# Weighting expert rows on ScalarE and adding them to the residual by accumulating DMAs, in place of two loads and VectorE additions

## Chip, cores and metric

The kernel runs on one core of a Trainium2 chip. The metric is the device time of one execution in microseconds (us). The time before is 1383.6 us, the median of three runs.

## What is computed

The reference is a two-layer decoder trunk for 256 tokens of width 1024, all in float32: a pooling mixer and a dense SwiGLU, then a gated DeltaNet and a mixture of experts, each added to a residual, and a last RMSNorm. The change touches the mixture of experts alone:

```
logits = t @ router_w + router_b                 # 256 tokens, 8 experts
top_vals, top_idx = top_k(logits, 2);  top_w = softmax(top_vals)
gates = sum(one_hot(top_idx) * top_w)            # (256, 8), two weights a row
for e in range(8):
    y = (silu(t @ w_gate[e]) * (t @ w_up[e])) @ w_down[e]     # inner width 3584
    out = out + gates[:, e:e+1] * y
h = h + out
```

## The kernel before

A float32 product is made of three passes of the faster fp32r format: each 128x1024 half of a weight tile is split into a rounded part `whi` (a cast on ScalarE) and a remainder `wlo` (a subtraction on VectorE, in `split`), and TensorE multiplies hi by hi, hi by lo and lo by hi. The pools of `whi` and `wlo` hold four halves each. Weight tiles of 1 MB come in through SyncE's queue into a ring of 16 raw tiles (six named `raw`, nine `raw_s`, one `raw_t`).

The experts are sorted by how many tokens chose them. When the counts allow it (`fit`, a branch at run time), the first four experts are computed on 128 gathered tokens each and the last four on 64 each (`FEW, SLIM = 4, 64`). An expert has seven chunks of 512 hidden columns. A chunk is a list of jobs, one for each weight half: eight for gate and up (`gate_up`), and four for down (`down`) that are run one chunk later, behind the gate and up jobs of the next chunk. Where an expert is 64 wide, hi and lo of the hidden rows lie side by side in one stationary tile, so a down job is four matmuls whose two halves land in rows 0 to 63 and 64 to 127 of PSUM bank `y0` or `y1`, and the two must be added.

`run` goes through the jobs in a loop: it first emits the split of job i + 3, then the matmuls of job i, then whatever was hung on job i with `after`. The class `Lane` keeps every engine's instructions in the order in which the program emits them (DMAs started from queues other than SyncE's are left out of that). So the copy that `put` makes of a finished expert stands in ScalarE's queue between two weight casts, and its addition stands in VectorE's queue between two subtractions:

```
ahead(i + 3)                   # cast on ScalarE, subtraction on VectorE
jobs[i][2](parts_.pop(i))      # matmuls
for f in post.pop(i, ()):      # put, where, fetch, gain, ...
    f()
```

`where(e)` finds out, by two small matmuls, in which row of a store in DRAM (`kept_rows`) each of the expert's rows belongs: a token's first choice in rows 1 to 256, its second choice in rows 257 to 512, empty rows beyond. `put(e, q)` runs for q = 0 behind the last down job of experts 0 to 6 and for q = 1 at the same job or two jobs later. It copies half q of the expert's output from PSUM to an SBUF tile `rows`; a 64-wide expert's second part is then added by VectorE. After q = 1 GpSimd scatters the tile to the store by an indirect DMA. In expert 7, behind chunks 3 and 4, `fetch(k)` loads the stored first and second choices through SyncE's queue into a raw tile, and `gain(k, tt)` adds them to the residual `h`, multiplied by the tokens' weights `w1` and `w2`, one VectorE instruction for each half of the tokens. Expert 7 itself is added to `h` by `scatter` at the end. `weights` makes the weights `w1`, `w2` and `gate` early in expert 0, one job ahead of the first `where`.

Of the kernel before, what the change touches and what calls it, by code (L numbers as in the profile page):

```python
# [9 lines left out]
F32 = mybir.dt.float32  # L10
F32R = mybir.dt.float32r
I32 = mybir.dt.int32
AF = mybir.ActivationFunctionType
ALU = mybir.AluOpType
# [3 lines left out]
P = 128  # L18
D = 1024
T = 256  # L20
# [194 lines left out]
def trunk(ctx: ExitStack, tc, x, gcol, win, prm, bc, cst, eye, pre, moe, out):  # L215
    nc = tc.nc
    held = {"on": False}
    pe, act, dve, pool, sp = [Lane(tc, e, held) for e in (nc.tensor, nc.scalar, nc.vector, nc.gpsimd, nc.sync)]
# [11 lines left out]
    kept_rows = store.tile([2 * T + 1 + P, D], F32, name="rows")  # L230

    h = cp.tile([P, 2, D], F32, name="h")
# [10 lines left out]
    HQ = [slice(0, 512), slice(512, 1024)]  # L243
# [32 lines left out]
    mhalf = cp.tile([P, 16], F32, name="mhalf")  # L276
# [11 lines left out]
    def raw_tile(dtype=F32):  # L288
        return wp.tile([P, UNIT], dtype, name="raw", bufs=RAWS["r"])
# [16 lines left out]
    def unit(src, i, dma=1, lo_engs=(None, None)):  # L306
        raw = load(src, i, dma)
        return [half(raw, s, lo_engs[s]) for s in range(2)]
# [263 lines left out]
    with esf:  # L572
# [30 lines left out]
        for j in range(1, 10):  # L603
            pg, pu_ = [(second, second_up)[k] if j == 1 else unit(pre, U_FFN + 3 * j + k) for k in range(2)]
# [6 lines left out]
        pg, pu_ = [unit(pre, U_FFN + 30 + k) for k in range(2)]  # L611
# [44 lines left out]
    kept = {}  # L656
# [579 lines left out]
    state, sel, xg, yps, cols = {}, {}, {}, {}, {}  # L1236

    def ms_bank(shape):
        return mps.tile(shape, F32, name="ms", bufs=2)

    def gu_bank(shape=(P, 512)):
        return mps.tile(list(shape), F32, name="gu", bufs=4)
# [4 lines left out]
    def half_mm(o, x_, s, hf, part, at, n, qs=(0, 1)):  # L1247

        (xh_, xl_), (hi, lo) = x_[hf], part
        for q in qs:  # L1250
            k, a = (at % 2) * 2 + q, slice(q * 512, q * 512 + 512)
            mm3(o, xh_[:, k, s], xl_[:, k, s], hi[:, a], lo[:, a], at == q == 0, at == n - 1 and q == 1)

    def sm(name, n=8):
        return mp.tile([P, 2, n], F32, name=name)
# [7 lines left out]
    m1, m2, ed, den, w1, w2 = [six[:, i] for i in range(6)]  # L1263
    lg, o1, o2, l2, gate, g2, rf = [sm(n_) for n_ in ("lg", "o1", "o2", "l2", "gate", "g2", "rf")]
# [112 lines left out]
    def width(e):  # L1377
        return state["width"].get(e, P)
# [37 lines left out]
    def where(e):  # L1416

        n = width(e)
        pw = ms_bank([P, 8])[:n]
        for tt in range(2):  # L1420
            pe.matmul(pw, state["Sp", e][:, tt, cols[e]], tid[:, tt, :], start=tt == 0, stop=tt == 1)
        spare = econ[:n, 6:7]
        dve.scalar_tensor_tensor(spare, pw[:, e:e + 1], 0.0, econ[:n, 3:4], op0=ALU.is_equal, op1=ALU.mult)
        dve.tensor_tensor(slot[:n, e:e + 1], spare, pw[:, e:e + 1], op=ALU.add)

    def put(e, q):
        if q == 0:
            state["put"] = state["rows"].tile([P, D], F32, name="rows", bufs=2)
        n, r, y = width(e), state["put"], yps[e][q]
        if n == P:  # L1430
            act.copy(r[:, HQ[q]], y)
        else:
            act.copy(r[:n, HQ[q]], y[n:2 * n])
            dve.tensor_add(r[:n, HQ[q]], r[:n, HQ[q]], y[:n])
        if q == 1:
            pool.indirect_dma_start(kept_rows, bass.IndirectOffsetOnAxis(ap=slot[:n, e:e + 1], axis=0), r[:n], None)

    def fetch(k):
        r = raw_tile().rearrange("p (t n) -> p t n", t=2)
        sp.dma_start(r, kept_rows[1 + k * T:1 + (k + 1) * T, :].rearrange("(t p) n -> p t n", t=2))  # L1440
        state["kept", k] = r

    def gain(k, tt):
        dve.scalar_tensor_tensor(h[:, tt], state["kept", k][:, tt], (w1, w2)[k][:, tt], h[:, tt], op0=ALU.mult, op1=ALU.add)

    def row_tile(dtype=F32):
        return state["tmp"].tile([P, 512], dtype, name="hm", bufs=2)
# [1 line left out]
    def opened(pg, n=P):  # L1449
        hm = row_tile()  # L1450
        act.activation(hm[:n], pg[:n], AF.Silu)
        return hm
# [83 lines left out]
    def expert_steps(block, few=0):  # L1536

        jobs, post = [], {}

        def after(i, f, *a):  # L1540
            post.setdefault(i, []).append(lambda: f(*a))

        def gate_up(e, c):
            at = len(jobs)
            dense = e == c == block == 0
            for i in range(4 if dense else 0, 8):
                w_, hf, s = i // 4, i // 2 % 2, i % 2

                def mm(part, w_=w_, hf=hf, s=s):
                    if hf == s == 0:  # L1550
                        state[e, w_] = gu_bank()
                    half_mm(state[e, w_][:width(e)], xg[e], cols[e], hf, part, 2 * hf + s, 4)
                jobs.append(((e, c * 4 + max(c - 1, 0) * 2 + 2 * w_ + hf), s, mm))

            def opening_():
                state["sg"] = opened(state[e, 0], width(e))

            def hidden():
                state["hm", e, c] = gated(state.pop("sg"), state[e, 1], width(e))
            if not dense:  # L1560
                after(at + 4, opening_)
            after(len(jobs) - 1, hidden)
            return at

        def down(e, c):
            at = len(jobs)
            base = (c + 2) * 4 + c * 2 if c < NCH - 1 else NCH * 4 + (NCH - 1) * 2
            final = e == NE - 1 and c == NCH - 1
            for fc in range(4):
                def mm(part, fc=fc):  # L1570
                    if c == fc == 0:
                        yps[e] = [mps.tile([P, 512], F32, name=f"y{q}") for q in range(2)]
                    st, sp_ = c == 0 and fc == 0, c == NCH - 1 and fc == 3
                    if final and fc == 3:
                        last_mm(e, c, part)
                    else:
                        down_mm(e, c, fc, part, (0, 1), st, sp_)
                jobs.append(((e, base + fc // 2), fc % 2, mm))
            if c == NCH - 1:
                for q in range(2):  # L1580
                    if not final and not block:
                        after(at + (3, 3 if e == 1 else 5)[q], put, e, q)
                    elif not final:
                        after(at + (3, 5)[q], out_split, e, q)
                        for tt in range(2):
                            after(at + (5, 7)[q], scatter, e, tt, q)
                if final:
                    for q in range(2):
                        for tt in range(2):
                            after(at + 3, scatter, e, tt, q)  # L1590
                    after(at + 3, lambda: close(state["g"]))
            return at

        def turn(e, c):
            state["hid", e, c] = hidden_T(state.pop(("hm", e, c)), (e, c) == (NE - 1, NCH - 1), width(e))

        prev, cut = None, 0
        for e in range(NE):
            for c in range(NCH):
                if (e, c) == (2, 0) and not block:  # L1600
                    after(len(jobs) - 3, turn, *prev)
                    down(*prev)
                    prev, cut = None, len(jobs)
                    for k in range(2):
                        after(cut + 4 + 4 * k, where, 2 + k)
                at = gate_up(e, c)
                if prev is not None:
                    after(at + (3 if c != 1 or e == 0 else TURN), turn, *prev)
                    down(*prev)
                if e % 2 == 1 and c == NCH - 1 and (block or e > 1) and e < NE - 1 - (few and 2):  # L1610
                    es_ = range(e + 1, NE if few and e + 1 == NE - few else e + 3)
                    after(at + 4, choose, es_)
                    for k, kc in zip((6, 7, 8, 9, 9, 10, 11, 11), range(KC)):
                        after(at + k, gather, es_, kc)
                    for k, e_ in enumerate(es_):
                        stays = block or e_ == NE - 1
                        after(at + 13 + 16 * k, back if stays else where, e_)
                if e == NE - 1 and not block and c in (3, 4):
                    after(at + 2, fetch, c - 3)
                    for tt in range(2):  # L1620
                        after(at + 8 + 2 * tt, gain, c - 3, tt)
                prev = e, c
        after(len(jobs) - 3, turn, *prev)
        down(*prev)
        return jobs, post, cut
# [188 lines left out]
```

## Time and profile before

| | |
|---|---|
| median of three runs | 1383.6 us (1383.38 to 1385.76) |
| the profiled execution | 1383.05 us, of which its span is 1381.3 us |
| granted TensorE clock | 0.996 of full speed |
| busy: TensorE / VectorE / ScalarE / GpSimd | 98% / 85% / 71% / 8% of the span |
| weights and the rest read from HBM | 420.11 MB, 309 GB/s over the span |

A matmul of 512 columns shows as 0.39 us long but the next one begins 0.23 us later, since matmuls overlap. An engine's record begins when it has what it waited for, so a late partner shows as a gap ahead of it.

### The profile page before, as it was taken

To read this page: it belongs to the slowest core of one execution; us is meant where nothing else is said; L and a number is where in the kernel's file an instruction comes from. 1 tells how busy PE (TensorE), PEld (TensorE's weight loads), DVE (VectorE), ACT (ScalarE), POOL (GpSimd) and SP (SyncE) were. 2 spreads that over 40 slices of the span, in tenths; PEclk is the share of its full clock that TensorE was granted. 3 is DMA by queue.
4 is the path that set the end of the run, shared out by engine and by line. 5 is a ranking of instruction groups with operands and counts; after the bars stand their busy time and mean duration, and the time that the engine had idled before them with its cause. 6 is when DMAs were issued, how large, how long until landed. Compare 5 with 4: busy or idle time off the path is not lost.

```text
span 1381.3 us, 19930 instructions
## 1 busy us (share of the span) xinstructions
PE 1349.6 (98%) x7149; PEld 1065.4 (77%) x7149; DVE 1171.3 (85%) x1473; ACT 983.0 (71%) x1298; POOL 114.4 (8%) x73
## 2 busy tenths in 40 slices
PE   8999999999998999999899999999999999999996
PEld 8999998989987888888788888876666666666654
DVE  5655556687888899999799999989999999999997
ACT  5544445752475787887688888788888888888875
POOL 0000001122331000000000000000004002201301
PEclk9999999999999999999999999999999999999999
DMA  9355551733319999999799999989999999997593
GB/s 384 153 214 187 195 196 63 292 121 100 116 58 390 395 371 376 379 382 374 304 360 376 374 373 382 376 335 386 404 389 406 421 408 406 413 409 294 230 428 158
DMA packets 60939, 427.51 MB, mean 310 GB/s; under 512 B 6880, under 2 KB 7136, under 8 KB 10400
## 3 DMA queue, kind: packets, MB, share of 16 engines
q1 hardware_dynamic: 59584, 422.75, 77.8%
q0 software_dynamic: 816, 2.88, 0.6%
q8 instruction: 58, 0.95, 0.3%
q10 hardware_dynamic: 432, 0.53, 0.1%
q14 instruction: 49, 0.40, 0.1%
HBM read 420.11 MB, written 6.03 MB: 309 GB/s over the span
## 4 chain that ended last, share of the span: by engine, by line
PE 89%; DVE 6%; issue 2%; ACT 1%; POOL 1%; DMA 0%; SPq 0%; ACTq 0%; POOLq 0%; DVEq 0%
PE gu L203 59%; PE y L203 17%; PE ya L203 9%; DVE wlo L203 4%; PE yq L203 2%; PE tp L203 1%; PE ms L203 1%; ACT whi L203 1%; PE gs L203 1%; DVE raw L203 0%; DVE h L203 0%; DVE rows L203 0%; DMA h<-in_x 0%; DVE hm L203 0%; DVE xl L203 0%
## 5 line engine op out<-in xcount | busy, mean ns | idle before, releaser
L203 DVE TENSOR_TENSOR wlo<-raw,whi 128x1024 fp32r<-128x1024 f32 x345 | 415.0, 1224 | 82.2 <-ACT whi L203 76.6
L203 DVE TENSOR_TENSOR wlo<-raw_s,whi 128x1024 fp32r<-128x1024 f32 x378 | 452.5, 1218 | 33.2 <-ACT whi L203 22.3
L203 ACT CAST whi<-raw_s 128x1024 fp32r<-128x1024 f32 x378 | 392.1, 1053 | 72.5 <-PE gu L203 54.1
L203 ACT CAST whi<-raw 128x1024 fp32r<-128x1024 f32 x346 | 357.9, 1051 | 106.4 <-PE gu L203 73.0
L203 PE MATMUL gu<-whi,xgh 128*128 128x512 f32 (+1 forms) x896 | 356.0, 397 | 3.6 <-DVE tl L203 3.6
L203 PE MATMUL gu<-wlo,xgh 128*128 128x512 f32 (+1 forms) x896 | 352.4, 393 | 3.2 <-DVE wlo L203 3.2
L203 PE MATMUL gu<-whi,xgl 128*128 128x512 f32 (+1 forms) x896 | 351.5, 392 | 0.0
L203 PEld LDWEIGHTS gu<-wlo,xgh 128*128 128x128 f32 (+1 forms) x896 | 144.9, 162 | 69.2 <-DVE wlo L203 15.5
L203 PEld LDWEIGHTS gu<-whi,xgh 128*128 128x128 f32 (+1 forms) x896 | 144.8, 162 | 60.5 <-issue 3.9
L203 PEld LDWEIGHTS gu<-whi,xgl 128*128 128x128 f32 (+1 forms) x896 | 144.8, 162 | 58.0
L203 PE MATMUL y<-wlo,th 128*128 128x512 f32 x328 | 128.9, 393 | 0.5 <-DVE wlo L203 0.3
L203 PE MATMUL y<-whi,th 128*128 128x512 f32 x328 | 128.4, 391 | 0.2 <-ACT th L203 0.2
L203 POOL DMA_INDIRECT rows<-rows,cmi x7 | 57.2, 8165 | 792.4 <-ACT rows L203 499.8
L203 PE MATMUL y<-whi,tl 128*128 128x512 f32 x336 | 113.1, 391 | 0.0
L203 PE MATMUL gu<-xh,wlo 128*128 128x256 f32 x320 | 90.1, 282 | 0.8 <-DVE wlo L203 0.8
L203 PE MATMUL gu<-xh,whi 128*128 128x256 f32 x320 | 90.2, 282 | 0.1
L203 PE MATMUL gu<-xl,whi 128*128 128x256 f32 x320 | 90.1, 281 | 0.0
L203 PEld LDWEIGHTS y<-wlo,th 128*128 128x128 f32 x328 | 61.7, 188 | 16.0 <-DVE wlo L203 3.8
L203 PEld LDWEIGHTS y<-whi,tl 128*128 128x128 f32 x336 | 63.1, 188 | 13.6
L203 PEld LDWEIGHTS y<-whi,th 128*128 128x128 f32 x328 | 61.6, 188 | 13.7 <-ACT th L203 0.6
L203 PEld LDWEIGHTS gu<-xh,wlo 128*128 128x128 f32 x320 | 61.4, 192 | 1.0 <-DVE wlo L203 1.0
L203 PEld LDWEIGHTS gu<-xh,whi 128*128 128x128 f32 x320 | 60.1, 188 | 0.6 <-ACT whi L203 0.3
(390 smaller groups left out, 1740.4 us busy)
## 6 DMA issues: line engine op xcount, KB each, us to landing
raw_s<-in_moe SPq DMA_DIRECT2D x189, 1024.0 KB, 7.1
raw<-in_moe SPq DMA_DIRECT2D x126, 1024.0 KB, 7.1
raw<-in_pre SPq DMA_DIRECT2D x56, 1024.0 KB, 4.9
raw_t<-in_moe SPq DMA_DIRECT2D x20, 1024.0 KB, 7.4
rows<-AB SPq DMA_DIRECT2D x2, 1024.0 KB, 6.5
raw<-rows SPq DMA_DIRECT2D x2, 1024.0 KB, 12.3
gbc<-in_bc SPq DMA_DIRECT2D x3, 512.0 KB, 9.1
h<-in_x SPq DMA_DIRECT2D x2, 512.0 KB, 4.1
```

The lines of the kernel that those rows point to most:

```text
L203: r = f(*a, **k)
```

## The change

Each stored row is multiplied by its weight before it is stored. `where` gets two more small matmuls, which pick the weights of the expert's rows out of `gate` in full float32, and a VectorE copy of them to a column of `mhalf`. `put` applies that column as the scale of ScalarE's activation: a 128-wide expert's copy out of PSUM becomes a scaled copy; for a 64-wide expert the copy and the addition stay and a scaled copy in place follows. `fetch` becomes a DMA of GpSimd's queue that adds 1 MB of the store to `h`, once for each choice, and `gain` is dropped.

```diff
         dve.tensor_tensor(slot[:n, e:e + 1], spare, pw[:, e:e + 1], op=ALU.add)
+        pg = ms_bank([P, 8])[:n]
+        for tt in range(2):
+            pe.matmul(pg, state["Sp", e][:, tt, cols[e]].bitcast(F32), gate[:, tt, :], start=tt == 0, stop=tt == 1)
+        dve.tensor_copy(mhalf[:n, 9 + e:10 + e], pg[:, e:e + 1])
 
     def put(e, q):
         if q == 0:
             state["put"] = state["rows"].tile([P, D], F32, name="rows", bufs=2)
-        n, r, y = width(e), state["put"], yps[e][q]
+        n, r, y = width(e), state["put"][:, HQ[q]], yps[e][q]
+        w = mhalf[:n, 9 + e:10 + e]
         if n == P:
-            act.copy(r[:, HQ[q]], y)
+            act.activation(r, y, AF.Copy, scale=w)
         else:
-            act.copy(r[:n, HQ[q]], y[n:2 * n])
-            dve.tensor_add(r[:n, HQ[q]], r[:n, HQ[q]], y[:n])
+            act.copy(r[:n], y[n:2 * n])
+            dve.tensor_add(r[:n], r[:n], y[:n])
+            act.activation(r[:n], r[:n], AF.Copy, scale=w)
+        r = state["put"]
         if q == 1:
             pool.indirect_dma_start(kept_rows, bass.IndirectOffsetOnAxis(ap=slot[:n, e:e + 1], axis=0), r[:n], None)
 
     def fetch(k):
-        r = raw_tile().rearrange("p (t n) -> p t n", t=2)
-        sp.dma_start(r, kept_rows[1 + k * T:1 + (k + 1) * T, :].rearrange("(t p) n -> p t n", t=2))
-        state["kept", k] = r
-
-    def gain(k, tt):
-        dve.scalar_tensor_tensor(h[:, tt], state["kept", k][:, tt], (w1, w2)[k][:, tt], h[:, tt], op0=ALU.mult, op1=ALU.add)
+        pool.dma_start(h, kept_rows[1 + k * T:1 + (k + 1) * T, :].rearrange("(t p) n -> p t n", t=2), accum_op=ALU.add)
...
                 if e == NE - 1 and not block and c in (3, 4):
                     after(at + 2, fetch, c - 3)
-                    for tt in range(2):
-                        after(at + 8 + 2 * tt, gain, c - 3, tt)
```

## Rows read from the trace of the kernel before

**Rows 1.** The page: busy us, share of the span, instructions of two engines.

```profile
PE 1349.6 (98%) x7149; PEld 1065.4 (77%) x7149; DVE 1171.3 (85%) x1473; ACT 983.0 (71%) x1298; POOL 114.4 (8%) x73
```

**Rows 2.** Windows: us, busy by engine (instructions), clock, DMA share, GB/s.

```profile
1266.40:1281.10 14.70, 14.64 (x65) 8.93 (x64) 14.70 (x17) 13.20 (x17) 8.62 (x1) 1.00 0.13 56
1173.70:1264.90 91.20, 91.20 (x403) 56.51 (x403) 87.91 (x84) 75.44 (x83) 7.70 (x1) 1.00 1.01 408
1297.50:1335.20 37.70, 34.45 (x151) 20.63 (x150) 36.98 (x36) 28.70 (x32) 0.00 (x0) 1.00 1.01 426
```

**Rows 3.** Timeline of TensorE, last down job behind expert 6's rows.

```profile
1280.65 0.39 PE L203 MATMUL y<-whi,th 128*128 128x512 f32 x1
1281.13 0.50 PE L203 MATMUL y<-wlo,th 128*128 128x512 f32 x1
```

**Rows 4.** Total waits of TensorE on VectorE's remainders, from 690 us on.

```profile
PE gu L203 <- DVE wlo L203: 3.2, 4, 1.1
```

**Rows 5.** Groups of VectorE from 450 us on: the additions of `gain`.

```profile
L203 DVE SCALAR_TENSOR_TENSOR h<-raw,six,h 128x1024 f32<-128x1024 f32 x4 | 5.1, 1269 | 0.0
```

**Rows 6.** Timeline of ScalarE where expert 6's rows are copied.

```profile
1266.60 0.58 ACT L203 COPY rows<-y 64x512 f32<-64x512 f32 x1
1267.09 2.00 ACT L203 CAST whi<-raw_s 128x1024 fp32r<-128x1024 f32 x2
1268.98 0.58 ACT L203 COPY rows<-y 64x512 f32<-64x512 f32 x1
1269.46 1.06 ACT L203 CAST whi<-raw_s 128x1024 fp32r<-128x1024 f32 x1
```

**Rows 7.** Timeline of VectorE in the same stretch.

```profile
1267.53 1.21 DVE L203 TENSOR_TENSOR wlo<-raw_s,whi 128x1024 fp32r<-128x1024 f32 x1
1268.67 0.67 DVE L203 TENSOR_TENSOR rows<-rows,y 64x512 f32<-64x512 f32 x1
1269.27 2.34 DVE L203 TENSOR_TENSOR wlo<-raw_s,whi 128x1024 fp32r<-128x1024 f32 x2
1271.54 0.67 DVE L203 TENSOR_TENSOR rows<-rows,y 64x512 f32<-64x512 f32 x1
```

**Rows 8.** Groups of ScalarE, whole span: count, busy us, mean ns, idle before.

```profile
L203 ACT COPY rows<-y 64x512 f32<-64x512 f32 x6 | 3.5, 584 | 0.1
...
L203 ACT ACTIVATE raw<-raw,st 128x512 f32<-128x512 f32 x2 | 1.3, 713 | 0.5 <-POOL st L203 0.5
```

**Rows 9.** Timeline of TensorE at a `where` of a 64-wide expert.

```profile
969.29 0.40 PE L203 MATMUL y<-wlo,th 128*128 128x512 f32 x1
...
969.61 0.47 PE L203 MATMUL y<-whi,th 128*128 128x512 f32 x1
```

**Rows 10.** Timeline of TensorE at `back(7)`: four matmuls in full float32.

```profile
989.53 0.39 PE L203 MATMUL gu<-whi,xgl 128*64 128x512 f32 x1
...
990.43 0.44 PE L203 MATMUL gu<-whi,xgh 128*64 128x512 f32 x1
```

**Rows 11.** Timeline around the first `where`: its matmuls, and `weights` on VectorE.

```profile
461.78 0.39 PE L203 MATMUL ms<-tid,Sp 128*128 128x8 f32 x2 [0.19 <-DVE tid L203]
...
462.02 0.48 PE L203 MATMUL gu<-whi,xgh 128*128 128x512 f32 x1
...
462.52 0.17 DVE L203 TENSOR_TENSOR gate<-gate,g 128x16 f32<-128x16 f32 x1
```

**Rows 12.** Timeline of GpSimd: the scatters of expert 3 and expert 6.

```profile
943.91 1.33 POOL L203 DMA_INDIRECT rows<-rows,cmi  x1 [120.76 <-ACT rows L203]
...
1272.48 17.32 POOL L203 DMA_INDIRECT rows<-rows,cmi  x1 [91.09 <-DVE rows L203]
```

**Rows 13.** Waits of SyncE's queue from 1200 us on: the scatter ahead of `fetch`.

```profile
SPq L203 <- DMA rows<-rows,cmi: 29.7, 1, 29.7
```

**Rows 14.** The page's DMA issues: count, KB each, us to landing.

```profile
raw<-rows SPq DMA_DIRECT2D x2, 1024.0 KB, 12.3
```

**Rows 15.** Timeline of VectorE: expert 7 is added to `h`.

```profile
1370.14 2.07 DVE L203 SCALAR_TENSOR_TENSOR h<-gu,gate,h 128x512 f32<-128x512 f32 x3
```

## The prediction

> **What bounds the kernel now.** I read the page first: TensorE is busy for 98% of the span, VectorE for 85% [rows 1]. That is an average over layers, so I cut the experts into windows. In a 64-wide expert between its seams TensorE has no idle time at all (91.20 of 91.20 us) and VectorE has 3.3 us of 91.2 to spare [rows 2]: TensorE bounds, with VectorE close behind. At the seam to the next expert, where `put` adds its two halves, the order turns: VectorE is busy for 14.70 of 14.70 us [rows 2]. The timeline of TensorE shows what that means: at the last down job of that stretch the second matmul begins 0.48 us after the first, where 0.23 us is usual, because its remainder is only just done [rows 3]. So VectorE's slack at a 64-wide seam is nil, and whatever delays VectorE there delays TensorE by as much. The seams behind experts 4 and 5 show the same sequence as the one behind expert 6; there are three. The third place is the stretch of `gain` in expert 7: 34.45 of 37.70 us of TensorE, so 3.25 us idle, against VectorE at 36.98 us [rows 2]. The list of waits agrees: 3.2 us in four waits on the remainders [rows 4].
>
> **What the removal gives.** The four additions took VectorE 5.1 us [rows 5] and made TensorE wait 3.2 us [rows 4]; the rest was in VectorE's slack. Without them the 3.2 us go: bounds 2.5 us, if a part of the lag comes from elsewhere, and 3.3 us, all the idle time of that window. The two loads gave SyncE's queue a wait of 29.7 us for the scatter [rows 13], with the weight loads behind it. This cost nothing: the DMA share fell to 0.13 [rows 2] while ScalarE's casts went on from the ring. So its removal gives nothing either.
>
> **What the scaled copies cost.** For the four 128-wide experts a copy becomes a scaled copy, once for once, on an engine with slack: nothing; without that cover eight times 713 - 584 ns [rows 8], 1.0 us. For the three 64-wide experts a third instruction stands in ScalarE's queue, and it waits for VectorE's addition. I follow it along the seam of expert 6. Today ScalarE copies at 1266.60 and goes straight to two casts at 1267.09 [rows 6], while VectorE is a step behind: it comes to the addition at 1268.67 and has the next two subtractions, whose casts are done, at 1269.27 [rows 7]. With the change ScalarE's queue stands still behind the copy. The addition still ends at 1268.67 + 0.67 = 1269.34. Then the scale begins about 0.04 us later and takes between 0.584 us (the copy of the same shape) and 0.713 us (twice the columns, with a scale operand) [rows 8]; I take 0.65. The next cast overlaps it by 0.1 us (two casts of 1.05 us take 2.00 [rows 6]), so it runs from 1269.93 to 1270.98, and its subtraction begins at 1271.01 in place of 1269.27: 1.74 us in which VectorE has nothing to do, with bounds of 1.67 and 1.80. Behind it are the casts and subtractions of the following jobs, and TensorE, which waits for them.
>
> The second half does it again: ScalarE's second copy comes after two casts, the second addition again stands behind both their subtractions, and the cast behind it is again not there. Nothing hides the one or the other, since this is the stretch with VectorE at 14.70 of 14.70 us [rows 2] and the lag that comes out of it ends in the wait of [rows 3]. Between seams nothing is given back, as TensorE is then the bound and what it lost is lost. Six holds of 1.74 us: 10.4 us, bounds 10.0 and 10.8. This is the largest term.
>
> **What `where` costs.** Seven calls get two matmuls in full float32 and a copy of one column. TensorE is the bound there, so the matmuls lie on the path. The pair in fp32r costs 969.61 - 969.29 - 0.23 = 0.09 us [rows 9]; that is the lower bound. The nearest in full float32 are the four matmuls of `back(7)`: 990.43 - 989.53 - 0.23 = 0.67 us [rows 10], or 0.34 us for two, with 128 columns where here there are 8, but half as wide a stationary tile as four of the seven calls have. I take 0.30 us, 2.1 us in all; bounds 0.6 us and 4.7 us (a whole 0.67 us each). The first call pays more: its first pair starts at 461.78 and the next job at 462.02, but `gate` is written by VectorE at 462.52 + 0.17 = 462.69 [rows 11], so the new pair stands in TensorE's queue until then: 0.75 us, bounds 0 and 0.9, with every later job behind it.
>
> The seven copies are put at nothing, since VectorE has a few per cent to spare between seams [rows 2]; without that cover they cost seven times about 0.15 us (the 0.17 us of a small VectorE instruction [rows 11]), 1.0 us.
>
> A rule of the Trainium skill sets a price of its own beside the rows of the float32 pair. "FP8 and Floating Point Precision", section "TensorE Precision Notes", says that a true float32 product takes four passes through the array. An estimate from it is four times the fp32r pair, 0.36 us a call and 2.5 us in all, and the sum below would be 1393.5 us. The trace so far agrees as to the order: four float32 matmuls cost 0.67 us where two of the other kind cost 0.09 us, but with other column counts; no row shows the new shape.
>
> **What the two DMAs cost.** They stand in GpSimd's queue behind the last scatter, which takes GpSimd 17.32 us for 64 rows [rows 12], and the second must wait for the first, since both add to `h`. They are on the path only if they end after the moment at which expert 7 is added to `h`: 1370.14 [rows 15], with the shift forecast here 1380. The last scatter is put off by three seams of 3.5 us and the 2.85 us of `where`, 13 us, and would end on GpSimd at about 1272.48 + 13 + 17.32 = 1303; with 3 us allowed for its rows to land, that leaves 74 us, or 37 us for each. A plain load of these rows took 12.3 us to land [rows 14]. If GpSimd needs for 256 rows twice the 1.33 us that 128 rows took it [rows 12], that is 15 us each, and 44 us are left over: nothing. The weights share the DMA engines at 426 GB/s in that stretch [rows 2], but their ring outlived 29.7 us without one load [rows 13], and 2 MB more are some 5 us at that rate.
>
> **The sum.** -3.2 + 10.4 + 2.1 + 0.75 = +10.05 us on the profiled execution's 1383.05 us: 1393.1 us. That execution lies 0.55 us below the median of the runs, within their spread of 2.4 us, and I leave the number there. The bounds add up to -3.3 + 10.0 + 0.6 + 0 = +7.3 and -2.5 + 10.8 + 4.7 + 0.9 + 1.0 (copies) + 1.0 (wide scaled copies) = +15.9, so 1390.4 to 1399 us.
>
> **The rivals.** (a) The holds are covered. The pools of `whi` and `wlo` are four deep, and two additions of 0.67 us already go through a seam at almost no loss; if the jobs split ahead bridged 1.74 us as well, the holds would cost nothing, and the time would be 1383.05 - 3.2 + 2.85 = 1382.7 us, or 1380.4 us with the cheapest `where`. The point that decides is the lead of VectorE's subtractions over TensorE's use of them in a seam: it would have to be over 1.7 us twice. For it: TensorE has a few jobs in hand at the seam's start. Against it: it is used up at the seam's end [rows 3]. Chance 0.10, and within 0.2% at its centre. (b) The accumulating DMAs land late. GpSimd took 17.32 us for 64 rows of a scatter but 1.33 us for 128 [rows 12]; if a DMA with accumulation goes the slow way, 256 rows are 69 us, with 12.3 us to land 82 us each, 164 us for two where 74 are free: 90 us late, 1483 us. It decides from 37 us each on. For it: one row in two. Against it: the slow ones are scatters of 64 rows, and these DMAs have 128 partitions and no indices. Chance 0.06. (c) The change does not reach the branch that runs: excluded, the copies of 64 rows are in the trace [rows 6]. A gain beyond (a) would need both a costless `where` and a fourth microsecond out of `gain`'s stretch, which has 3.25 us to give: 0.02, with the rest, 0.82, for the forecast.
>
> **How the numbers follow.** The likeliest is 1393.1 us. Its own range, 1390 to 1399 us, holds most of its 0.82. To hold the time 8 times in 10 I widen it to 1387 below, for holds that are covered in part (one of the two at each seam covered: -5.2 us, 1387.9 us), and to 1400 above; (a) and (b) stay outside with 0.16 together. A measurement of this kernel tells about 0.2% (2.8 us) from no change. Slower by more: the forecast and (b), 0.88. Within: nearly all of (a), 0.09. Faster: 0.03.
>
> **What would show it.** At the three 64-wide seams the new copy in place should follow the addition at once, the cast behind it begin some 2.8 us later than now against the copy ahead, VectorE be idle for about 1.7 us twice with ScalarE's cast as the releaser, and TensorE idle for about 3.5 us a seam. In expert 7's chunks 3 to 5 TensorE should have no idle time. The first `where` should show TensorE waiting for `gate`. SyncE's queue should have no wait of 29.7 us, and the second accumulating DMA should land well ahead of the additions of expert 7. The prediction is wrong if VectorE's idle time at the seams does not reach TensorE, or if the last additions to `h` wait for a DMA.

## The result: 0.8% slower, with VectorE's new gaps at the seams as the cause

The changed kernel takes 1395.34 us (median of four runs, 1394.45 to 1395.74) where the kernel before took 1383.9 us (median of four, 1383.38 to 1385.76): a ratio of 1.0078, with a 95% interval of 1.0066 to 1.0091. (The ratios in this text are not the quotients of the two medians, here 1.0083, and differ from them by up to 0.07%: differences under 1 us are read from the traces alone.) The forecast was 1393.1 us. The profiled execution took 1395.56 us with a span of 1393.8 us, 12.5 us more than the profiled execution before.

The page answers to [rows 1]; its columns are busy us, share of the span and instructions.

```profile
PE 1355.7 (97%) x7177; PEld 1067.8 (77%) x7177; DVE 1168.5 (84%) x1476; ACT 986.7 (71%) x1304; POOL 67.7 (5%) x75
```

TensorE has 28 records and 6.1 us more, ScalarE six instructions and 3.7 us more, VectorE 2.8 us less, GpSimd 47 us less. None of these is the 12.5 us; the stretches have to be looked at. The first window is the seam behind expert 6, from the same matmul to the same matmul as in [rows 2]; the second is the stretch where `gain` stood, somewhat widened (us, busy by engine, clock, DMA share, GB/s).

```profile
1279.03:1297.35 18.32, 15.48 (x65) 8.76 (x64) 14.87 (x17) 14.50 (x19) 2.23 (x2) 1.00 0.92 339
1309.00:1352.00 43.00, 43.00 (x191) 26.71 (x190) 41.66 (x40) 35.73 (x40) 1.22 (x1) 1.00 1.02 399
```

The stretch of `gain` has lost all its idle time of TensorE (43.00 of 43.00 us). The seam, with the same 65 matmuls and 17 instructions of VectorE, has grown from 14.70 to 18.32 us; TensorE is busy for 15.48 of them and VectorE for 14.87, neither of them full. An engine that was full at the seam before and now is not has been made to wait. ScalarE's timeline at this seam says for what; it answers to [rows 6] (start, us, engine, operation, shapes, and in brackets the idle time ahead and who ended it).

```profile
1279.23 0.58 ACT L203 COPY rows<-y 64x512 f32<-64x512 f32 x1
1282.00 0.73 ACT L203 ACTIVATE rows<-rows,mhalf 64x512 f32<-64x512 f32 x1 [2.18 <-DVE rows L203]
1282.63 1.98 ACT L203 CAST whi<-raw_s 128x1024 fp32r<-128x1024 f32 x2
1284.51 0.58 ACT L203 COPY rows<-y 64x512 f32<-64x512 f32 x1
1286.68 0.72 ACT L203 ACTIVATE rows<-rows,mhalf 64x512 f32<-64x512 f32 x1 [1.58 <-DVE rows L203]
```

Behind each copy ScalarE stands still, 2.18 and 1.58 us, until VectorE's addition is done; then it scales, and only then casts. VectorE's timeline, which answers to [rows 7], shows the other half of it.

```profile
1281.30 0.67 DVE L203 TENSOR_TENSOR rows<-rows,y 64x512 f32<-64x512 f32 x1
1283.69 2.36 DVE L203 TENSOR_TENSOR wlo<-raw_s,whi 128x1024 fp32r<-128x1024 f32 x2 [1.73 <-ACT whi L203]
1285.97 0.67 DVE L203 TENSOR_TENSOR rows<-rows,y 64x512 f32<-64x512 f32 x1
1288.37 3.50 DVE L203 TENSOR_TENSOR wlo<-raw_s,whi 128x1024 fp32r<-128x1024 f32 x3 [1.73 <-ACT whi L203]
```

Before, a subtraction followed 0.60 us behind the addition's start (1268.67 to 1269.27 in [rows 7]); now it follows 2.39 us behind it, because its cast is not there: 1.79 us lost. The second half loses as much: 2.40 us in place of 0.59, as before the subtraction behind the second addition (1271.54 in [rows 7]) began here:

```profile
1272.13 3.48 DVE L203 TENSOR_TENSOR wlo<-raw_s,whi 128x1024 fp32r<-128x1024 f32 x3
```

TensorE takes over both losses in full. The matmul of [rows 3] that began at 1281.13 is now the second of these rows of TensorE's timeline:

```profile
1284.97 0.45 PE L203 MATMUL gu<-wlo,xgh 128*64 128x512 f32 x1 [0.82 <-DVE wlo L203]
...
1297.38 0.50 PE L203 MATMUL y<-wlo,th 128*128 128x512 f32 x1 [0.55 <-DVE wlo L203]
```

ScalarE's first copy at this seam is 12.63 us later than before (1266.60 to 1279.23), and this matmul 16.25 us: the seam costs 3.6 us. The list of TensorE's waits for split weights from 1040 us on shows the same (us in total, times, longest). Before, it had the four waits of `gain`'s stretch [rows 4] and one that [rows 4] leaves out, of 0.4 us behind expert 7; that one is still among the four of the last line, so 8.6 us of these waits are at the three seams:

```profile
PE gu L203 <- DVE wlo L203: 4.9, 6, 0.8
PE gu L203 <- ACT whi L203: 2.1, 6, 0.4
PE y L203 <- DVE wlo L203: 2.0, 4, 0.5
```

To find where the rest went I set the starts of matching matmuls of the two profiled executions against each other, and read where the difference between them grows:

| place | growth, us |
|---|---|
| ahead of the experts | +0.53 |
| first `where` | +1.19 |
| the six other `where`, 0.38 to 0.44 each | +2.52 |
| gathers at 683 to 691 us, behind the run-time branch | +1.13 |
| the three seams: 3.61, 3.58, 3.64 | +10.83 |
| `gain`'s stretch, mostly in four steps: 1.22, 0.65, 1.24, 0.64 | -3.82 |

The rows add up to +12.4 of the 12.5 us. The first row and the gathers belong to no part of the change; the gathers are taken up below.

### The profile page after: what moved, and what is told of

It is laid out like the page before. It is cut to its first block, busy times and chain, and to the rows that moved or that the text cites. A ratio compares the mean times of both kernels' runs of the same rounds, so it can differ in the third digit from the quotient of the medians.

```text
span 1393.8 us, 20014 instructions
## 1 busy us (share of the span) xinstructions
PE 1355.7 (97%) x7177; PEld 1067.8 (77%) x7177; DVE 1168.5 (84%) x1476; ACT 986.7 (71%) x1304; POOL 67.7 (5%) x75
## 4 chain that ended last, share of the span: by engine, by line
PE 91%; DVE 5%; ACT 2%; issue 1%; POOL 1%; DMA 0%; SPq 0%; ACTq 0%; POOLq 0%; DVEq 0%
PE gu L203 60%; PE y L203 18%; PE ya L203 9%; DVE wlo L203 3%; PE yq L203 2%; PE ms L203 1%; PE tp L203 1%; ACT whi L203 1%; PE gs L203 1%; DVE raw L203 0%; DMA h<-in_x 0%; DVE h L203 0%; DVE xl L203 0%; ACT xh L203 0%; POOL st L203 0%
## 5 line engine op out<-in xcount | busy, mean ns | idle before, releaser
L203 PEld LDWEIGHTS gu<-xl,whi 128*128 128x128 f32 x320 | 60.1, 188 | 0.4
## 6 DMA issues: line engine op xcount, KB each, us to landing
h<-rows POOLq DMA_DIRECT2D x2, 1024.0 KB, 15.5
```

Of the source, the lines that this page charges most:

```text
L203: r = f(*a, **k)
```

## The experiments

Each median stands beside that of the kernel before, timed in the same series on the same chip.

**The hold alone.** The scaled copy in place is put into the kernel before, with a column of ones as the scale; no other part of the change is made.

```diff
+    dve.memset(mhalf[:, 15:16], 1.0)
...
             dve.tensor_add(r[:n, HQ[q]], r[:n, HQ[q]], y[:n])
+            act.activation(r[:n, HQ[q]], r[:n, HQ[q]], AF.Copy, scale=mhalf[:n, 15:16])
```

> The kernel before with one addition: behind each VectorE addition of a 64-wide expert, ScalarE copies the tile in place with a scale of 1.0. No new matmuls, and the loads and gains stay. Theory (ScalarE's queue is held by its wait for VectorE, six times, and VectorE at the seams has nothing to spare): 3.6 us a seam as in the changed kernel's trace, 10.8 us in all, so about 1394.7 us against 1383.9; two VectorE gaps of about 1.7 us at each 64-wide seam. Rival 1 (the cost in the changed kernel comes mostly from the float32 matmuls and the DMAs; the four-deep pools cover the holds): under 2 us.

Measured: 1394.61 against 1384.04 us, ratio 1.0072 (1.0058 to 1.0086). VectorE's timeline at the seam of expert 6 has the same two gaps, with the same releaser:

```profile
1274.66 0.67 DVE L203 TENSOR_TENSOR rows<-rows,y 64x512 f32<-64x512 f32 x1
1277.06 2.36 DVE L203 TENSOR_TENSOR wlo<-raw_s,whi 128x1024 fp32r<-128x1024 f32 x2 [1.73 <-ACT whi L203]
1279.33 0.67 DVE L203 TENSOR_TENSOR rows<-rows,y 64x512 f32<-64x512 f32 x1
1281.73 2.36 DVE L203 TENSOR_TENSOR wlo<-raw_s,whi 128x1024 fp32r<-128x1024 f32 x2 [1.73 <-ACT whi L203]
```

Six instructions of 0.73 us cost 10.6 us. Nearly all of the change's loss is here. The starts of matching matmuls say the same: 3.63 or 3.64 us at each of the three seams and nothing at the other places of the change.

**The same instruction without the wait.** Is it ScalarE's time or its standing still? The same number of scaled copies of the same shape, but each reads PSUM and stands ahead of the addition.

```diff
+    dve.memset(mhalf[:, 15:16], 1.0)
...
             act.copy(r[:n, HQ[q]], y[n:2 * n])
+            act.activation(r[:n, HQ[q]], y[n:2 * n], AF.Copy, scale=mhalf[n:2 * n, 15:16])
             dve.tensor_add(r[:n, HQ[q]], r[:n, HQ[q]], y[:n])
```

> The kernel before, where for 64-wide experts ScalarE makes the copy out of PSUM twice, the second time as a scaled copy with a scale of 1.0, ahead of VectorE's addition: an instruction more of about 0.6 us at the same places, but none that waits for VectorE. Theory (the wait costs, not the work): within 0.7 us of the kernel before, about 1384 us, no VectorE gap over 0.5 us at the seams. Rival 2 (ScalarE's extra work is what delays the casts): six times 0.6 to 0.7 us or more, 1388 us and up.

Measured: 1383.95 against 1384.04 us, ratio 0.9996 (0.9987 to 1.0005). ScalarE's timeline at the same seam, and VectorE's below it:

```profile
1265.99 0.58 ACT L203 COPY rows<-y 64x512 f32<-64x512 f32 x1
1266.61 0.69 ACT L203 ACTIVATE rows<-y,mhalf 64x512 f32<-64x512 f32 x1
1267.32 2.00 ACT L203 CAST whi<-raw_s 128x1024 fp32r<-128x1024 f32 x2
```

```profile
1268.05 0.67 DVE L203 TENSOR_TENSOR rows<-rows,y 64x512 f32<-64x512 f32 x1
1268.64 2.35 DVE L203 TENSOR_TENSOR wlo<-raw_s,whi 128x1024 fp32r<-128x1024 f32 x2
```

The third instruction itself is nearly free: 0.13 to 0.15 us a seam by the starts of matching matmuls. The cast comes 1.33 us behind the copy, where 0.49 us was usual [rows 6], and still ahead of VectorE, which goes from the addition to its subtraction in 0.59 us as before. What costs is that ScalarE's queue waits for VectorE.

**`where` alone.** The new part of `where` is put into the kernel before; its result is not used.

```diff
+        pg = ms_bank([P, 8])[:n]
+        for tt in range(2):
+            pe.matmul(pg, state["Sp", e][:, tt, cols[e]].bitcast(F32), gate[:, tt, :], start=tt == 0, stop=tt == 1)
+        dve.tensor_copy(mhalf[:n, 9 + e:10 + e], pg[:, e:e + 1])
```

> The kernel before with the new part of where alone: seven pairs of float32 matmuls and the copy of one column, whose result nobody uses. Theory, from the shift of TensorE's matmuls between the two traces (1.19 us at the first call, 0.38 to 0.44 us at each of the six others): 3.7 us, about 1387.6 us. By the prediction's own term: 2.85 us, 1386.8 us. Rival 1 (the matmuls cost most of the change): 8 us or more.

Measured: 1388.09 against 1384.04 us, ratio 1.0025 (1.0016 to 1.0034). By the starts of matching matmuls the first call costs 1.19 us and the others 0.39 to 0.45, 3.7 us in all; the gathers behind the branch add 0.8. The same calls of the changed kernel, first and second, in TensorE's timeline:

```profile
462.30 0.38 PE L203 MATMUL ms<-tid,Sp 128*128 128x8 f32 x2 [0.19 <-DVE tid L203]
463.27 0.61 PE L203 MATMUL ms<-gate,Sp 128*128 128x8 f32 x4 [0.58 <-DVE gate L203]
463.74 0.48 PE L203 MATMUL gu<-whi,xgh 128*128 128x512 f32 x1
...
465.21 0.28 PE L203 MATMUL ms<-tid,Sp 128*128 128x8 f32 x2
465.34 0.59 PE L203 MATMUL ms<-gate,Sp 128*128 128x8 f32 x4
465.79 0.48 PE L203 MATMUL gu<-whi,xgh 128*128 128x512 f32 x1
```

Before, the job behind the first call began 0.24 us behind its first matmul [rows 11]; now it is 1.44 us, so 1.20 more. At the second call the new pair holds TensorE from 465.34 to 465.79. Two matmuls in full float32 show as four records here.

**The accumulating DMAs alone.** `fetch` adds the store to `h`, `gain` is dropped, and the rows are stored unweighted: this kernel leaves the experts' weights out of all but the last expert.

```diff
-        r = raw_tile().rearrange("p (t n) -> p t n", t=2)
-        sp.dma_start(r, kept_rows[1 + k * T:1 + (k + 1) * T, :].rearrange("(t p) n -> p t n", t=2))
...
+        pool.dma_start(h, kept_rows[1 + k * T:1 + (k + 1) * T, :].rearrange("(t p) n -> p t n", t=2), accum_op=ALU.add)
...
```

> The kernel before, with the two loads and the four VectorE additions replaced by the two accumulating DMAs, and nothing else: the rows are stored and added without their weights. Theory, from the shift of TensorE's matmuls in expert 7's chunks 3 to 5: -3.8 us, about 1380.1 us; by the prediction's term -3.2 us. With the scatter of 64 rows again released by a VectorE that has no gap, its 17.3 us on GpSimd come back and the accumulating DMAs start after it, still over 40 us ahead of their use. Rival 3 (the accumulating DMAs take from the weight loads what the additions gave back): no change, 1383 to 1385 us.

Measured: 1379.9 against 1384.04 us, ratio 0.9963 (0.9949 to 0.9976). In the window of `gain`'s stretch TensorE has no idle time:

```profile
1297.00:1334.00 37.00, 37.00 (x163) 22.56 (x162) 35.88 (x35) 30.76 (x34) 2.57 (x2) 1.00 1.03 364
```

The three parts by their medians are +10.6, +4.05 and -4.1 us, +10.5 in sum, where the whole change measured +11.4. By the ratios it is 8.3 of 10.8 us. Each interval is up to 2 us wide to either side, so the times say that no large fourth part is missing, no more. The starts of matching matmuls are sharper: 10.9 us at the seams, 3.7 at `where` and -3.8 in `gain`'s stretch in the three kernels, the same as in the whole change to 0.1 us.

**The scale without the wait, within the change.** The first part is scaled as ScalarE copies it, the second as VectorE adds it.

```diff
-            act.copy(r[:n], y[n:2 * n])
-            dve.tensor_add(r[:n], r[:n], y[:n])
-            act.activation(r[:n], r[:n], AF.Copy, scale=w)
+            act.activation(r[:n], y[n:2 * n], AF.Copy, scale=w)
+            dve.scalar_tensor_tensor(r[:n], y[:n], w, r[:n], op0=ALU.mult, op1=ALU.add)
```

> The changed kernel without the holds: for 64-wide experts ScalarE's copy out of PSUM is itself scaled, and VectorE adds the other part scaled, in one instruction, so that nothing on ScalarE waits for VectorE. Theory: the changed kernel's 1395.3 less the 10.6 us that the holds alone cost, plus six times 0.07 us, as VectorE's multiply-add of 512 columns took 0.744 us where its addition took 0.672: about 1385 us; the 64-row scatters, released by VectorE again, take some 17 us on GpSimd again. Rival 2 (scaling costs wherever it is done): 1390 us or more.

Measured: 1384.31 against 1383.93 us, ratio 1.0000 (0.9991 to 1.0009). Without the hold the rest of the change is worth nothing that can be measured: what `gain` gave, `where` takes.

**The instruction kept, but moved.** The scaled copy in place stays as the change has it, emitted three jobs later, with the scatter behind it.

```diff
...
+    def weigh(e, q):
+        n, r = width(e), state["put"][:, HQ[q]]
+        if n < P:
+            act.activation(r[:n], r[:n], AF.Copy, scale=mhalf[:n, 9 + e:10 + e])
+            send(e, q)
...
                         after(at + (3, 3 if e == 1 else 5)[q], put, e, q)
+                        after(at + (6, 8)[q], weigh, e, q)
```

> The changed kernel with the very same scaled copies in place, each emitted three jobs later in ScalarE's queue, so that the addition is done when ScalarE comes to it. Theory (the wait costs): about 1385 us, at most 1387, since ScalarE's extra 0.73 us now lies in its waits for TensorE. Rival 2 (the instruction itself costs): stays above 1390 us.

Measured: 1383.49 against 1383.93 us, ratio 0.9993 (0.9984 to 1.0001). ScalarE's timeline at the seam of expert 6 has the instruction, with no wait ahead of it, as the addition (1273.22 to 1273.89) is done 1.08 us earlier:

```profile
1273.54 0.58 ACT L203 COPY rows<-y 64x512 f32<-64x512 f32 x1
1274.02 1.06 ACT L203 CAST whi<-raw_s 128x1024 fp32r<-128x1024 f32 x1
1274.97 0.72 ACT L203 ACTIVATE rows<-rows,mhalf 64x512 f32<-64x512 f32 x1
1275.59 2.07 ACT L203 CAST whi<-raw_s 128x1024 fp32r<-128x1024 f32 x2
```

The same work on the same engines, with its place in the queue moved, gives back about 12 us (1395.34 to 1383.49, each beside 1383.9 of the kernel before); the seams cost 0.01 to 0.02 us each. One of this kernel's twelve executions took 4748 us; it is not in the ratio, and why it did stays open.

**The weights beside the row numbers.** To the scale of the last but one kernel comes a `where` without float32 matmuls: `gate` is split into a rounded part and a remainder, which stand as 16 more columns beside the row numbers in `tid`, VectorE adds the two products, and the first two calls come one job later.

```diff
...
-        pw = ms_bank([P, 8])[:n]
+        pw = ms_bank([P, 24])[:n]
...
-        pg = ms_bank([P, 8])[:n]
-        for tt in range(2):
-            pe.matmul(pg, state["Sp", e][:, tt, cols[e]].bitcast(F32), gate[:, tt, :], start=tt == 0, stop=tt == 1)
-        dve.tensor_copy(mhalf[:n, 9 + e:10 + e], pg[:, e:e + 1])
+        w = mhalf[:n, 9 + e:10 + e]
+        dve.tensor_copy(w, pw[:, 8 + e:9 + e])
+        dve.tensor_tensor(w, w, pw[:, 16 + e:17 + e], op=ALU.add)
...
-            post.setdefault(9 + k, []).append(lambda k=k: where(k))
+            post.setdefault(10 + k, []).append(lambda k=k: where(k))
```

> The version with both parts scaled at the copy, and where made cheap: gate is split into an fp32r part and its remainder, both stand beside the row numbers in the moving operand of the matmuls that were there before (24 columns in place of 8), VectorE adds the two picked columns, and the first where comes one job later, behind the making of gate. Theory: the accumulating DMAs keep their 4.1 us, the 4.0 us of where fall to under 0.7 us, and the multiply-adds cost 0.4 us: about 1381 us, faster than the kernel before by 0.1 to 0.25%. Rival (the price of where is VectorE's copies and the wait at the first call, not the float32 matmuls): no better than 1384 us.

Measured: 1381.84 against 1383.93 us, ratio 0.9987 (0.9978 to 0.9996). TensorE's timeline at the second call shows the pair of 24 columns starting 0.24 us behind one matmul and giving way to the next after 0.14 us:

```profile
464.41 0.40 PE L203 MATMUL gu<-whi,xgl 128*128 128x512 f32 x1
464.65 0.28 PE L203 MATMUL ms<-tid,Sp 128*128 128x24 f32 x2
464.79 0.48 PE L203 MATMUL y<-whi,th 128*128 128x512 f32 x1
```

**Both mended.** This `where` and the scale three jobs later.

> Both mends together: the scaled copies in place three jobs later, and the weights picked beside the row numbers with fp32r columns, the first where one job later; the accumulating DMAs as in the change. Theory: the 4.1 us of the accumulating DMAs stay nearly whole, about 1380.5 us, ratio 0.997 to 0.998. Rival (something of the new put or where is left on the path): 1382 us or more, no better than the version with both parts scaled.

Measured: 1382.14 against 1383.14 us, ratio 0.9989 (0.998 to 0.9998). So the change can be made to gain, but only about 0.1%. That misses the expectation of 1380.5 us and lies where its rival put it, but the rival's reason is not in the trace: by the starts of matching matmuls the seams cost 0.02 to 0.03 us each, all `where` together 0.2 us, and `gain`'s stretch gives its 3.8 us. The medians are of executions at several mean granted clocks: the ones at 0.997 took 1378.44 us with this kernel (mean of two) and 1381.84 us with the kernel before (mean of seven), 3.4 us apart. Eight of this kernel's eleven executions ran at 0.992 or 0.993, but three of fifteen of the kernel before; whether this kernel brings the low clock about is not shown.

**The wait for `gate`.** The changed kernel with its first two `where` one job later, run once.

```diff
-            post.setdefault(9 + k, []).append(lambda k=k: where(k))
+            post.setdefault(10 + k, []).append(lambda k=k: where(k))
```

> The changed kernel with its first two calls of where one job later each, so that gate is written before TensorE comes to the float32 pair. Theory (the first call's price is 0.42 us for the matmuls and 0.75 us for the wait): TensorE's shift behind the first call falls from 1.2 us to about 0.4, and the list of waits has no wait for gate. Rival (the first float32 pair is dear by itself, say from a switch of format): the shift stays near 1.2 us.

Measured: 1395.6 us. A single run cannot show a microsecond, but the trace can: the wait for `gate` is gone, and the list of waits has a smaller one of the second call in its place:

```profile
PE ms L203 <- DVE mhalf L203: 0.3, 1, 0.3
```

The first call now delays the matmul behind it by 0.45 us, as the other calls do, so its float32 pair is not dear by itself. Over both calls the matmuls come 1.04 us late against the kernel before, where they were 1.63 us late in the changed kernel: 0.6 us came back, with the smaller wait still in it.

## Why the prediction was right, step by step

**What bounds the kernel** held: VectorE at the seams, TensorE elsewhere. The hold alone lost 10.6 us and an instruction of nearly the same length without the wait lost next to nothing; and what VectorE loses at a seam, 1.79 and 1.81 us, is what TensorE loses there, 3.6 us, as it must be where VectorE is full.

**The scaled copies.** The mechanism came out as followed on paper, and the size nearly: 1.79 and 1.81 us lost a half in VectorE's timeline where 1.74 was worked out, and 10.83 us over six holds in the shift of the matmuls where 10.4 was. The difference is the scale in place, 0.725 us where 0.65 was taken; the row with twice the columns, 0.713 [rows 8], was the better price, since it had the same form (a scale operand), while the copy had the same shape. Rival (a), four-deep pools that bridge the holds, is refuted by the hold alone. Half of it was true: the pools cover two additions and even a third instruction on ScalarE, as the copy without a wait shows, but not a wait that goes round from one engine to the other.

**`where`** was mis-sized low: the pair was taken at 0.30 us and measured 0.42 on average (2.52 / 6), and the first call at 1.05 us and measured 1.19; 3.7 us in place of 2.85. The first call's wait itself was right: it is 1.19 - 0.42 = 0.77 us from start to start (the list shows a gap of 0.58), and 0.75 was predicted. The rule of the Trainium skill ("FP8 and Floating Point Precision", section "TensorE Precision Notes": a true float32 product takes four passes) gave 0.36 us, nearer than my choice from rows with other column counts; the trace agrees with it as to the kind, at 0.42 us.

**The removal** was mis-sized too. It gave 3.8 us (4.1 by the accumulating DMAs alone), outside the bounds of 2.5 and 3.3. The failed step is the bound "all the idle time of that window". These rows of the kernel before, from TensorE's timeline in `gain`'s stretch, show why:

```profile
1312.81 0.40 PE L203 MATMUL gu<-whi,xgh 128*64 128x512 f32 x1
1314.35 0.44 PE L203 MATMUL gu<-wlo,xgh 128*64 128x512 f32 x1 [1.14 <-DVE wlo L203]
```

From start to start are 1.54 us. Without a wait it would be 0.23, so 1.31 us are lost; the gap is shown as 1.14, since it is counted from the end of a matmul that lasts 0.40 us in the record but lets the next one in after 0.23. Each wait is read some 0.16 us too short in this way, four of them 0.64 us, and 3.2 + 0.64 = 3.84 us is about the 3.8 us that came back. I knew the 0.23 us and used it in [rows 3], but took the windows' idle time as a limit all the same. The 8.6 us of waits at the seams for 10.83 us lost are the same kind of reading.

**The DMAs** cost nothing, as predicted, and rival (b) is refuted. GpSimd's timeline in the changed kernel:

```profile
1287.67 0.89 POOL L203 DMA_INDIRECT rows<-rows,cmi  x1 [111.15 <-ACT rows L203]
...
1293.91 1.34 POOL L1446 DMA_DIRECT2D h<-rows  x1 [5.34 <-DMA rows<-rows,cmi]
1310.72 1.22 POOL L1446 DMA_DIRECT2D h<-rows  x1 [15.47 <-DMA h<-rows]
```

The page's line of DMA issues has both (KB each, us from issue to landing):

```profile
h<-rows POOLq DMA_DIRECT2D x2, 1024.0 KB, 15.5
```

The second is issued when the first has landed and is done at about 1310.72 + 15.5 = 1326 us, more than 50 us ahead of the first addition of expert 7 to `h` at 1382.6. A launch of 256 rows took GpSimd 1.34 and 1.22 us, where the scatter of 128 took 1.33 [rows 12], and the sums took 15.5 us to land where a plain load took 12.3 [rows 14].

**In sum** three terms were 0.4 us too low, 0.85 us too low and 0.6 us too high (10.83, 3.71 and -3.82 against 10.4, 2.85 and -3.2): +10.7 in place of +10.05. That they partly cancel is luck: the first two alone come to 1.3 us, which would still have been inside the range. The rest of the 12.5 us between the profiled executions is the start (0.53) and the gathers (1.13), which the prediction did not have.

## What to carry to other kernels

An instruction that waits for another engine costs the time for which its own queue stands, and that reaches the end of the kernel when the queue feeds an engine that is full: 0.73 us of work cost 1.8 us each time, and next to nothing three jobs later or when folded into the copy ahead. So where an edit adds a step to a chain that goes from one engine to another and back, look first for the place in the queue at which its input is already there. And lost time of TensorE is read from start to start: gaps behind modelled ends come out too short by the overlap of two matmuls.

## What had not been expected of the hardware

**A scatter's time on GpSimd goes with what VectorE does beside it.** In the kernel before GpSimd took 17.32 us for a scatter of 64 rows [rows 12], in the changed kernel 0.89. The scatter of expert 6 in the kernel before ends at 1272.48 + 17.32 = 1289.80 us, and VectorE's first listed gap in that stretch is this one:

```profile
1289.55 1.22 DVE L203 TENSOR_TENSOR wlo<-raw,whi 128x1024 fp32r<-128x1024 f32 x1 [0.18 <-ACT whi L203]
```

The same holds for the two scatters ahead of it: gaps of about 0.18 us that end at 1072.72 and 1181.14, scatters that end at 1072.98 and 1181.40. In the changed kernel and in the one with the hold alone VectorE stands for 1.73 us just as the scatter is issued, and all six take about 0.9 us; with the scale in both parts, where VectorE has no such gap, they take 17.3 again. A rule of the Trainium skill bears on it: "SBUF — State Buffer", section "Who interferes with whom", says that VectorE and GpSimd share a pair of ports that one of them holds for a whole instruction, and that a VectorE instruction with two inputs in SBUF, as the subtractions are, contends with a GpSimd instruction that reads SBUF. The gaps at which these scatters end agree with it. But VectorE also ran instructions with one input in PSUM during the 17 us (`th<-gu,th` and `hm<-hm,gu`), which that rule does not name, and the scatter stayed. In other kernels it did not: with the accumulating DMAs alone two scatters take 7.65 us and end 0.24 to 0.26 us behind the start of the subtraction that follows `hm<-hm,gu`, without a listed gap; with the scale three jobs later they take 2.4 us and end 0.50 to 0.53 us behind the one that follows a `th` or `tl`. With the copy twice they take 1.75 us beside neither. So that the ports are the cause is not shown, and what decides stays open. In this kernel none of it reaches the end, as nobody needs the rows soon.

**The granted clock behind a wait is not the same in every execution.** At the run-time branch TensorE waits 2.55 us for VectorE in the kernel before, and 2.54 to 2.72 in the others, and then gathers. The windows behind that wait, of the kernel before,

```profile
683.00:686.00 3.00, 2.85 (x11) 2.56 (x12) 1.19 (x4) 1.17 (x3) 0.00 (x0) 0.51 0.20 81
```

of the kernel with the hold alone, whose code is the same up to there,

```profile
683.00:686.00 3.00, 2.21 (x16) 1.80 (x15) 1.53 (x4) 2.26 (x5) 0.00 (x0) 1.00 0.11 44
```

and of the changed kernel

```profile
686.00:689.00 3.00, 2.55 (x14) 2.21 (x12) 1.82 (x3) 2.07 (x4) 0.00 (x0) 0.64 0.00 0
689.00:691.00 2.00, 1.52 (x7) 1.36 (x7) 1.01 (x3) 0.47 (x2) 0.00 (x0) 0.50 0.34 53
```

have a granted clock of 0.51, 1.00, and 0.64 then 0.50: half speed is 1.2 of 2.4 GHz. The low clock lasts longer in the changed kernel, and this is the 1.13 us of the gathers in the table. Such stretches go with the spread of the runs: beside the kernel with the scale in both parts, executions of the kernel before with a mean granted clock of 0.997 took 1381.7 us and those with 0.992 took 1385.3 us (means of three and of eleven). Whether the float32 pair of `where` has to do with it stays open: in all five profiled executions with the pair the clock falls behind the first gather, as here; in the six without it, it falls at once (the kernel before, the accumulating DMAs alone) or not at all (the four others). One profile of each is too few to tell, but the timed executions go the same way: of 38 with the pair (the one of 4748 us left out) none had a mean clock of 0.996 or more, of 108 without it 28 had. But `where` also brings the branch some 1.5 to 2 us later, so it is not shown that the pair itself is the reason.
